# Expert weights in 4 KB runs, hidden sums chunk by chunk, a second tile's work in seven pieces

## The chip, the cores and the metric

One core of a Trainium2 chip runs the whole kernel in one launch. The metric is the time of the program on the device in microseconds, as the median of several runs. TensorE (PE) multiplies, ScalarE (ACT), VectorE (DVE) and GpSimd (POOL) do the rest, SP issues most loads; the five engines run their own queues in order and meet at semaphores.

## The reference

One layer over 1024 latent tokens and 256 context tokens, width 1024. Attention and a gated token mixer come first (they are not touched). Then a mixture of experts (MoE): each token goes to 2 of 16 experts, and

```python
for e in range(N_EXPERTS):                              # 16
    hid = silu(t @ w1[e]) * (t @ w3[e])                 # w1, w3: 1024 x 512
    out = out + gate[:, e:e + 1] * (hid @ w2[e])        # w2: 512 x 1024
```

All inputs are float32. Each expert has 6 MB of weights.

## The kernel before, in words

**Split operands.** A float32 product is made as three matmuls (`mm3`, lines 85 to 88): the operand's part `hi`, rounded by a copy on ACT, and the rest `lo`, which a subtraction gives, combined as hi x hi, hi x lo and lo x hi. So each weight is converted: `e_hi` (line 941, ACT) and `e_lo` (line 946, DVE or POOL).

**Chunks.** An expert's weights come in six chunks of 1 MB, numbered g = 6e + c. Chunks 0 to 3 hold 512 rows of w1 and w3, 256 columns of each, so that (c // 2) is the half `f` of the hidden columns and (c % 2) the half of the rows; a run in memory is 1 KB. Chunks 4 and 5 are w2, in runs of 4 KB. There are seven buffers for raw chunks (`raw`) and six for converted ones (`chi`, `clo`). `e_conv` converts one half of a chunk (1024 columns) at a time; when the second half is done, the next load into that buffer is issued on SP. Some second halves, and both of chunk 7, go to POOL.

**Tiles.** A routing stage writes each expert's list of tokens; `cr[e]` holds their number in registers of all engines (`count`, line 1462). A first tile of up to 128 tokens is always computed. If there are more, a second tile is computed, as a full one (over 192 tokens) or as a half one, whose `hi` and `lo` parts stand side by side in one stationary operand, which makes two matmuls of three (`half_h`, `half_y`). The last expert may have a third tile (`more`).

**One tile.** `gather` (POOL) fetches the tokens' rows; `x_split` transposes them on PE in blocks of 128 consecutive columns (line 1345) and splits them; `h_mm(e, j, f)` adds up one half of the hidden columns over all eight row blocks, 24 matmuls (ACT and DVE then make the hidden part); `h_T` transposes the hidden part; `y_mm` makes 24 matmuls with w2; `y_out` scales and scatters with an add (POOL, line 1388; a half tile at line 1451).

**Order.** The MoE's order is written out by hand for every engine (`manual_schedule`, lines 1534 to 1586). For an expert: the second tile's x (`x_more`, jumped over when there is none; the jump is recorded at line 1564), `h_mm` of half 0, the gather of the next expert's second tile, two conversions, the rest of the second tile as one piece (`more1`, jumped over at line 1528), then half 1 of the first tile, the next expert's x, and the first tile's y. Conversions stand between these. PSUM has four banks for `yb`, two for the hidden sums and two (`pst`) for the transposes. A jump is one compare and branch on every engine; a piece that is jumped over leaves behind it, on each engine that had work in it, an event that adds up the semaphore steps left out.

Of the kernel before, what the change touches and what calls it, by code (L numbers as in the profile page):

```python
# [39 lines left out]
def hybrid_layer_kernel(ctx, tc, a, out):  # L40
# [887 lines left out]
    def e_conv(g, i, eng=None):  # L928
        if g >= CH:
            return  # L930
        e_hi(g, i)
        if eng is None:
            eng = nc.gpsimd if g == 7 or i == 1 and (g == 6 or g >= 2 * 6 and g % 6 in (0, 5)) else nc.vector
        e_lo(g, i, eng)

    def e_hi(g, i):
        sl = slice(i * 1024, (i + 1) * 1024)
        if g == 7:
            nc.vector.tensor_copy(chi[g % NS][:, sl], raw[slot_of(g)][:, sl])
        else:  # L940
            nc.scalar.activation(chi[g % NS][:, sl], raw[slot_of(g)][:, sl], AF.Copy)  # L941

    def e_lo(g, i, eng):
        sl = slice(i * 1024, (i + 1) * 1024)
        r, hi, lo = raw[slot_of(g)], chi[g % NS], clo[g % NS]
        eng.tensor_tensor(lo[:, sl], r[:, sl], hi[:, sl].bitcast(F32), op=ALU.subtract)  # L946
        if i == 1:
            e_load(g + NR if g > 1 else g + 3)
# [215 lines left out]
    for t in range(NT - 1):  # L1164
# [12 lines left out]
        if t >= 5:  # L1177
            e_conv(t - 5, 0)
            e_conv(t - 5, 1)
# [51 lines left out]
    def x_part(src, w, first, last, ks):  # L1231
        for k in ks:
            nc.tensor.matmul(xg[k // 4][:, k % 4, :], src[:, k * P:(k + 1) * P], w, start=first and k % 4 == 0, stop=last and k % 4 == 3)
# [73 lines left out]
    def wk(e, c, k):  # L1307
        g = 6 * e + c
        n = 512 if c < 4 else 1024
        return chi[g % NS][:, k * n:(k + 1) * n], clo[g % NS][:, k * n:(k + 1) * n]  # L1310
# [9 lines left out]
    def bank4(j):  # L1320
        return bank(j, pst).rearrange("p (a n) -> p a n", a=4)
# [5 lines left out]
    hA = ep.tile([P, 256], F32, name="hA")  # L1327
    hB = ep.tile([P, 256], F32, name="hB")
# [9 lines left out]
    def x_split(j):  # L1338
        xg = (sc_f, xgi, xg2)[min(j, 2)]
        hi, lo = (xTi, xT0)[min(j, 1)]  # L1340
        for q in range(2):
            tr = bank4(j)
# [7 lines left out]
    def h_mm(e, j, f, hook=None):  # L1350
        hi, lo = (xTi, xT0)[min(j, 1)]
        po = bank(j, psh)
        for k in range(KD):
            wh, wl = wk(e, 2 * f + k // 4, k % 4)
            mm3(po, hi[:, k, :], lo[:, k, :], wh, wl, k == 0, k == KD - 1)
            if hook is not None and k == hook[0]:
                hook[1]()
        h = (hA, hB)[min(j, 1)]
        nc.scalar.activation(h, po[:, 0:256], AF.Silu)
        nc.vector.tensor_tensor(h, h, po[:, 256:512], op=ALU.mult)  # L1360

    def h_T(j, f):
        hi, lo = hTs[min(j, 1)]
        h = (hA, hB)[min(j, 1)]
        tr = bank4(j)
        for i in range(2):
            nc.tensor.transpose(tr[:, i, :], h[:, i * P:(i + 1) * P], ident)  # L1367
        sl = slice(f * 2, f * 2 + 2)
        nc.scalar.activation(hi[:, sl, :], tr[:, 0:2, :], AF.Copy)
        nc.vector.tensor_tensor(lo[:, sl, :], tr[:, 0:2, :], hi[:, sl, :].bitcast(F32), op=ALU.subtract)  # L1370

    def y_mm(e, j, k0, k1):
        hi, lo = hTs[min(j, 1)]
        if k0 == 0:
            yss[j] = [bank(1, psy) for _ in range(2)]
        for k in range(k0, k1):
            wh, wl = wk(e, 4 + k // 2, k % 2)
            for i in range(2):
                sl = slice(i * 512, (i + 1) * 512)
                mm3(yss[j][i], hi[:, k, :], lo[:, k, :], wh[:, sl], wl[:, sl], k == 0, k == 3)  # L1380

    def y_out(e, j):
# [20 lines left out]
    def half_x(j):  # L1403
        xg = (xgi, xg2)[j - 1]
        for q in range(2):
            tr = bank4(1)
            for i in range(4):
                k = q * 4 + i
                nc.tensor.transpose(tr[:, i, 0:HP], xg[0:HP, k * P:(k + 1) * P], ident[0:HP, 0:HP])
            half_split(xT0[0][:, q * 4:q * 4 + 4, :], tr)  # L1410

    def half_h(e, j, f, hook=None):
        po = bank(1, psy)
        for k in range(KD):
            wh, wl = wk(e, 2 * f + k // 4, k % 4)
            nc.tensor.matmul(po, xT0[0][:, k, :], wh, start=k == 0, stop=False)
            nc.tensor.matmul(po, xT0[0][:, k, :], wl, start=False, stop=k == KD - 1)
            if hook is not None and k == hook[0]:
                hook[1]()
        s = xg2[0:HP, f * 512:(f + 1) * 512]  # L1420
        half_sum(s, po)
        h = hB[0:HP, :]
        nc.scalar.activation(h, s[:, 0:256], AF.Silu)
        nc.vector.tensor_tensor(h, h, s[:, 256:512], op=ALU.mult)

    def half_hT(f):
        tr = bank4(1)
        for i in range(2):
            nc.tensor.transpose(tr[:, i, 0:HP], hB[0:HP, i * P:(i + 1) * P], ident[0:HP, 0:HP])
# [259 lines left out]
```

## Time and profile before

| what | value |
|---|---|
| median of 3 runs (lowest, highest) | 1068.88 us (1066.27, 1072.99) |
| the profiled execution: its time, its span | 1073.15 us, 1071.3 us |
| busy in the span: PE, DVE, ACT, POOL | 1004.6, 735.4, 536.3, 381.6 us |
| mean granted TensorE clock | 0.984 of full speed |
| moved by DMA | 255.26 MB, mean 238 GB/s |
| MoE: first hidden matmul, last matmul | 606.3 us, 1052.8 us |

By the timeline experts 1, 3 to 9 and 14 have one tile; 10, 11, 13 and 15 have a full second one, 0, 2 and 12 a half second one, and 15 a half third one as well. PE's busy time contains the overlap of a matmul's filling with the one before it: a matmul of 512 columns is recorded with 0.39 us, but the next starts 0.23 us later. So gaps are read from the starts. A share of busy time is a mean over stages with different limits; the MoE is read by itself.

### The profile page before, as it was taken

The page shows a single profiled execution, that of the slowest core. Times are in us where ns is not written, and L with a number is a line of the kernel's source. Part 1 is how long each engine was busy: PE and PEld are TensorE (multiplying, and loading weights), DVE is VectorE, ACT ScalarE, POOL GpSimd, SP SyncE. Part 2 cuts the span into 40 slices and gives each one's busy share as a digit, 9 for nine tenths or more (in the row PEclk, how much of TensorE's full clock was granted, in tenths as well). Part 3 has the DMA queues.
Part 4 walks back from the last instruction along what each step waited for, and adds up shares of the span by engine and source line. Part 5 has one row for each costly group of instructions (what it writes and reads, how often), then busy time and mean ns, then how long its engine had stood idle before and what let it go on. Part 6 is the DMA issues. An engine that isn't in the chain of part 4 may idle for free. (4 is left out here: it accounts for less than half of the span.)

```text
span 1071.3 us, 15841 instructions
## 1 busy us (share of the span) xinstructions
PE 1004.6 (94%) x5161; PEld 816.6 (76%) x5161; DVE 735.4 (69%) x1478; ACT 536.3 (50%) x1024; POOL 381.6 (36%) x311
## 2 busy tenths in 40 slices
PE   9999899999999999999999888999998999999992
PEld 4688787876888989988888766777776888787771
DVE  2677658874627989967776858688888654765821
ACT  4643125243527989854322437476676543554611
POOL 1130321232302565641223554435645423243510
PEclk9999999999999999999999999999999999999997
DMA  9793605876757797959342698799999996886431
GB/s 325 271 316 134 200 1 177 287 237 243 252 210 263 253 352 265 322 182 324 122 149 80 202 299 287 247 332 353 346 360 353 343 294 201 292 257 194 131 60 16
DMA packets 138118, 255.26 MB, mean 238 GB/s; under 512 B 10310, under 2 KB 86726, under 8 KB 137994
## 3 DMA queue, kind: packets, MB, share of 16 engines
q1 hardware_dynamic: 122876, 201.57, 55.7%
q0 software_dynamic: 15120, 52.19, 16.1%
q8 instruction: 60, 0.98, 0.4%
q14 instruction: 62, 0.51, 0.2%
HBM read 210.45 MB, written 43.29 MB: 237 GB/s over the span
## 5 line engine op out<-in xcount | busy, mean ns | idle before, releaser
L946 DVE TENSOR_TENSOR clo<-raw,chi 128x1024 fp32r<-128x1024 f32 x140 | 174.2, 1291 | 18.8 <-ACT chi L941 17.7
L941 ACT ACTIVATE chi<-raw 128x1024 fp32r<-128x1024 f32 x166 | 162.6, 1049 | 1.5 <-DMA raw<-in_w 1.3
L86 PE MATMUL po<-whi,hhi 128*128 128x512 f32 x352 | 146.0, 415 | 0.0
L87 PE MATMUL po<-wlo,hhi 128*128 128x512 f32 x352 | 139.6, 397 | 0.0
L88 PE MATMUL po<-whi,hlo 128*128 128x512 f32 x352 | 139.3, 396 | 0.0
L1388 POOL DMA_INDIRECT out<-xb,lt x20 | 58.0, 2899 | 152.0 <-DVE xb L1387 152.0
L86 PE MATMUL b<-chi,yhi 128*128 128x512 f32 x256 | 104.7, 409 | 7.0 <-PEq L1528 4.1
L88 PE MATMUL b<-chi,ylo 128*128 128x512 f32 x256 | 101.7, 397 | 2.0 <-DVE ylo L1348 1.6
L87 PE MATMUL b<-clo,yhi 128*128 128x512 f32 x256 | 101.3, 396 | 0.0
L83 POOL TENSOR_TENSOR ss<-ss,nhalf 128x1 f32<-128x1 f32 (+1 forms) x36 | 46.0, 1276 | 144.2 <-DVE ss L82 144.0
L946 POOL TENSOR_TENSOR clo<-raw,chi 128x1024 fp32r<-128x1024 f32 x26 | 75.2, 2899 | 52.1 <-ACT chi L941 27.8
L86 PEld LDWEIGHTS po<-whi,hhi 128*128 128x128 f32 x352 | 66.7, 189 | 16.6 <-issue 2.6
L87 PEld LDWEIGHTS po<-wlo,hhi 128*128 128x128 f32 x352 | 66.8, 190 | 16.0 <-issue 2.4
L88 PEld LDWEIGHTS po<-whi,hlo 128*128 128x128 f32 x352 | 66.7, 189 | 15.9 <-DVE hlo L218 0.3
L86 PEld LDWEIGHTS b<-chi,yhi 128*128 128x128 f32 x256 | 48.4, 189 | 23.4 <-issue 8.4
L86 PE MATMUL yb<-chi,hhi 128*128 128x512 f32 x160 | 65.7, 411 | 0.0
L88 PE MATMUL yb<-chi,hlo 128*128 128x512 f32 x160 | 62.8, 393 | 0.0
L87 PE MATMUL yb<-clo,hhi 128*128 128x512 f32 x160 | 62.6, 391 | 0.0
L88 PEld LDWEIGHTS b<-chi,ylo 128*128 128x128 f32 x256 | 48.5, 190 | 14.1 <-DVE ylo L1348 2.1
L770 DVE TENSOR_TENSOR PT<-tr,PT 128x384 fp32r<-128x384 f32 (+1 forms) x128 | 56.4, 483 | 3.3 <-ACT PT L764 3.2
L87 PEld LDWEIGHTS b<-clo,yhi 128*128 128x128 f32 x256 | 48.5, 189 | 9.6
L572 DVE CUSTOM_DVE_ANT_0 S<-S,bt 128x640 f32<-128x640 f32 x64 | 52.7, 824 | 4.2 <-DMA bt<-in_btab 3.9
(316 smaller groups left out, 2343.7 us busy)
## 6 DMA issues: line engine op xcount, KB each, us to landing
raw<-in_w SPq DMA_DIRECT2D x104, 512.0 KB, 8.2
raw<-in_w SPq DMA_DIRECT2D x27, 1024.0 KB, 9.4
wraw<-in_w_ada SPq DMA_DIRECT2D x32, 512.0 KB, 5.1
v<-vD SPq DMA_DIRECT2D x16, 768.0 KB, 6.3
bt<-in_btab SPq DMA_DIRECT2D x32, 384.0 KB, 6.8
wraw<-in_w_in SPq DMA_DIRECT2D x20, 512.0 KB, 5.4
acc<-in_w SPq DMA_DIRECT2D x18, 512.0 KB, 7.4
wada<-in_w_ada SPq DMA_DIRECT2D x16, 512.0 KB, 6.6
```

The lines of the kernel that those rows point to most:

```text
L83: nc.gpsimd.tensor_tensor(r, r, nhalf[:, :n], op=ALU.pow)
L86: nc.tensor.matmul(po, xh, wh, start=first, stop=False)
L87: nc.tensor.matmul(po, xh, wl, start=False, stop=False)
L88: nc.tensor.matmul(po, xl, wh, start=False, stop=last)
L572: nc.vector.tensor_tensor_reduce(sv, sv, btl[t, h // 2][:, h % 2 * 384:h % 2 * 384 + LK], op0=ALU.add, op1=ALU.max, scale=1.0, scalar=-3e3 ...
L770: nc.vector.tensor_tensor(lo, tr, hi.bitcast(F32), op=ALU.subtract)
L941: nc.scalar.activation(chi[g % NS][:, sl], raw[slot_of(g)][:, sl], AF.Copy)
L946: eng.tensor_tensor(lo[:, sl], r[:, sl], hi[:, sl].bitcast(F32), op=ALU.subtract)
L1388: nc.gpsimd.indirect_dma_start(out=out[:, :], out_offset=bass.IndirectOffsetOnAxis(ap=lt[:, e, j, 0:1], axis=0), in_=y, in_offset=None, co ...
```

## The change

Weights w1 and w3: partition p takes rows 8p to 8p + 7, and chunk c holds two of them (2c and 2c + 1), with all 512 columns, in runs of 4 KB. The hidden sums of both halves `f` then need all four chunks, and they are taken chunk by chunk, six matmuls for each half. So row block k of x consists of every eighth column, and the transposes read x so (`cols`). A chunk is converted whole (2048 columns) by ACT and DVE, chunk 7 of each six in two halves; POOL converts nothing any more but one half of chunk 3, ahead of the MoE (line 1289, as before). The second tile of an expert is taken in seven pieces, each with its own jump: its x, its hidden sums after each chunk of the first tile (four pieces), its hidden transposes, and its y. For expert 0 its x and hidden sums are one piece. A third tile (`alone`) uses the same parts in an order of its own.

```diff
-                eng.dma_start(r.rearrange("p (k n) -> p k n", k=4)[:, :, i * 256:(i + 1) * 256],
-                                  a[w][e, (c % 2) * 512:(c % 2) * 512 + 512, (c // 2) * 256:(c // 2) * 256 + 256].rearrange("(k p) n -> p k n", p=P))
+                eng.dma_start(r[:, i * 1024:(i + 1) * 1024],
+                              a[w][e].rearrange("(p k) n -> p (k n)", k=KD)[:, c * 1024:(c + 1) * 1024])
...
+    def e_conv(g):
         if g >= CH:
             return
-        e_hi(g, i)
-        if eng is None:
-            eng = nc.gpsimd if g == 7 or i == 1 and (g == 6 or g >= 2 * 6 and g % 6 in (0, 5)) else nc.vector
-        e_lo(g, i, eng)
+        e_hi(g, None)
+        e_lo(g, None, nc.vector)
...
+    def w13(e, f, k):
+        g = 6 * e + k // 2
+        return [w[g % NS].rearrange("p (m k n) -> p m k n", m=2, k=2)[:, :, k % 2, f * 256:(f + 1) * 256] for w in (chi, clo)]
+
+
+    def cols(x, k):
+        return x.rearrange("p (n k) -> p k n", k=KD)[:, k, :]
...
-                nc.tensor.transpose(tr[:, i, :], xg[:, k * P:(k + 1) * P], ident)
+                nc.tensor.transpose(tr[:, i, :], cols(xg, k), ident)
...
+    def h_part(e, j, half, f, chunks):
         hi, lo = (xTi, xT0)[min(j, 1)]
+        for k in range(2 * chunks[0], 2 * chunks[-1] + 2):
+            if k == 0 and j != 1:
+                pos[j, f] = bank(j, psh)
+            po = pos[j, f]
+            wh, wl = w13(e, f, k)
+            if half:
+                nc.tensor.matmul(po, hi[:, k, :], wh, start=k == 0, stop=False)
+                nc.tensor.matmul(po, hi[:, k, :], wl, start=False, stop=k == KD - 1)
+            else:
+                mm3(po, hi[:, k, :], lo[:, k, :], wh, wl, k == 0, k == KD - 1)
+        if chunks[-1] == 3:
...
+            nc.scalar.activation(h, s[:, 0:256], AF.Silu)
+            nc.vector.tensor_tensor(h, h, s[:, 256:512], op=ALU.mult)
...
+    def alone(e, j, half):
+        for c in range(3):
+            for f in range(2):
+                h_part(e, j, half, f, [c])
+        h_part(e, j, half, 0, [3])
+        h_T(e, j, half, 0)
+        h_part(e, j, half, 1, [3])
+        y_mm(e, j, half, 0)
+        h_T(e, j, half, 1)
+        for k in range(1, 4):
+            y_mm(e, j, half, k)
+        y_out(e, j, half)
...
+    def expert(e):
+        g0 = 6 * e
+
+        def second(f, *a):
+            with tc.If(cr[e] > P):
+                with tc.If(cr[e] > P + HP) as c:
+                    f(False, *a)
+                with c.Else():
+                    f(True, *a)
...
+        def second_T(half):
+            for f in range(2):
+                h_T(e, 1, half, f)
+
+        def second_y(half):
+            for k in range(4):
+                y_mm(e, 1, half, k)
+            y_out(e, 1, half)
...
+        if e:
+            second(second_x)
+            gather_more(e + 1)
+        for c in range(3):
+            if e or c:
+                conv(4 + c if e else 3 + c)
+            if e and c == 2:
+                e_hi(g0 + 7, 0)
+            chunk(0, False, c)
+            if e:
+                second(second_h, [c])
+        h_part(e, 0, False, 0, [3])
+        if e:
+            e_lo(g0 + 7, 0, nc.vector)
+        h_part(e, 0, False, 1, [3])
+        if e:
+            second(second_h, [3])
+        else:
+            second(second_xh)
+            gather_more(1)
+            conv(6)
+            e_hi(7, 0)
+            e_lo(7, 0, nc.vector)
+        h_T(e, 0, False, 0, bank(1, psy))
+        if e + 1 < E:
+            x_split(0)
+        if e + 2 < E:
+            gather(e + 2, 0)
+        y_mm(e, 0, False, 0)
+        h_T(e, 0, False, 1)
+        second(second_T)
+        e_hi(g0 + 7, 1)
+        e_lo(g0 + 7, 1, nc.vector)
+        conv(8)
+        for k in range(1, 4):
+            y_mm(e, 0, False, k)
+        y_out(e, 0, False)
+        yss[1] = [bank(1, psy) for _ in range(2)]
+        if e == E - 1:
+            with tc.If(cr[e] > P * 2):
+                gather(e, 2)
+        second(second_y)
+        conv(9)
...
     for e in range(E):
         if e + 1 < E:
-            x_split(0)
...
+            count(e + 1)
+        expert(e)
```

## Rows read from the trace of the kernel before

**Rows 1.** Windows by stage: length, busy time by engine, clock, DMA share, GB/s

```profile
700.00:820.00 120.00, 112.26 (x507) 87.16 (x506) 103.05 (x109) 83.73 (x110) 63.93 (x24) 1.00 1.06 348
820.00:840.00 20.00, 17.53 (x76) 13.90 (x75) 12.88 (x17) 10.97 (x16) 10.74 (x5) 0.91 1.07 352
840.00:983.00 143.00, 141.07 (x658) 113.78 (x656) 86.21 (x111) 70.33 (x104) 48.32 (x23) 1.00 0.82 255
```

**Rows 2.** Waits: ACT conversions for landed weights; TensorE's: total us, times, longest

```profile
  DMA raw<-in_w: 1.3, 1
...
PE b L1367 <- DVE ylo L1348: 5.1, 6, 0.9
PE b L86 <- PEq L1528: 4.1, 2, 2.5
```

**Rows 3.** Timeline of TensorE, one expert with one tile: start, us, instruction

```profile
740.38 0.47 PE L86 MATMUL b<-chi,yhi 128*128 128x512 f32 x1
...
745.58 0.40 PE L87 MATMUL b<-clo,yhi 128*128 128x512 f32 x1
745.82 0.39 PE L88 MATMUL b<-chi,ylo 128*128 128x512 f32 x1
746.36 0.47 PE L86 MATMUL b<-chi,yhi 128*128 128x512 f32 x1
...
752.18 1.03 PE L1345 MATMUL b<-ident,gf 128*128 128x128 f32 x8
...
755.43 0.44 PE L1367 MATMUL b<-ident,hA 128*128 128x128 f32 x2 [0.82 <-DVE ylo L1348]
...
760.17 0.47 PE L86 MATMUL b<-chi,yhi 128*128 128x512 f32 x1
```

**Rows 4.** Lines 1528, 1564, 1462 on TensorE's sequencer: ns min/median/max, first, last start

```profile
L1528 PEldq COMPARE_BRANCH  x15: 65/325/6158, 649.3 to 1004.9; - x15
L1528 PEldq EVENT_SEMAPHORE  x9: 51/51/51, 653.3 to 988.9; - x9
...
L1564 PEldq EVENT_SEMAPHORE  x9: 51/51/51, 645.0 to 982.9; - x9
...
L1462 PEldq TENSOR_LOAD <-cnt x17: 297/304/489, 608.0 to 999.6; - x17
```

**Rows 5.** Scatters: page, part 5, and groups by line

```profile
L1388 POOL DMA_INDIRECT out<-xb,lt x20 | 58.0, 2899 | 152.0 <-DVE xb L1387 152.0
...
L1451 POOL DMA_INDIRECT out<-xb,lt x4 | 5.8, 1447 | 42.0 <-DVE xb L1450 42.0
```

**Rows 6.** VectorE: line 946 by itself; timeline in the expert of rows 3

```profile
L946 DVE TENSOR_TENSOR clo<-raw,chi x140: 1206/1220/3415, 489.3 to 1012.9; 128x1024 fp32r<-128x1024 f32 x140
...
751.96 2.48 DVE L946 TENSOR_TENSOR clo<-raw,chi 128x1024 fp32r<-128x1024 f32 x1 [0.21 <-ACT chi L941]
...
754.69 1.27 DVE L1348 TENSOR_TENSOR ylo<-b,yhi 128x512 fp32r<-128x512 f32 x2
```

**Rows 7.** Timeline of TensorE behind the longest jump

```profile
828.39 0.63 PE L87 MATMUL b<-clo,yhi 128*128 128x512 f32 x1
828.82 0.63 PE L88 MATMUL b<-chi,ylo 128*128 128x512 f32 x1
```

**Rows 8.** Timeline of half tiles: TensorE in expert 12, ACT and TensorE in the third

```profile
928.19 0.31 PE L1429 MATMUL yb<-ident,hB 64*128 64x64 f32 x2 [0.74 <-DVE hB L1424]
...
1047.26 0.59 ACT L1396 ACTIVATE yb<-yb 64x512 f32<-64x512 f32 x1 [0.33 <-PE yb L1417]
...
1049.62 0.30 PE L1429 MATMUL yb<-ident,hB 64*128 64x64 f32 x2 [0.18 <-DVE hB L1424]
1050.67 0.50 PE L1440 MATMUL yb<-chi,hhi 128*128 128x512 f32 x1 [0.75 <-DVE hhi L1401]
```

**Rows 9.** Timeline of VectorE at the end of a half tile's y

```profile
935.00 0.68 DVE L1397 TENSOR_TENSOR yb<-yb 64x512 f32<-64x512 f32 x1 [2.44 <-ACT yb L1396]
...
937.09 0.74 DVE L1450 SCALAR_TENSOR_TENSOR xb<-yb,lt,gf 64x512 f32<-64x512 f32 x1
```

**Rows 10.** Line 1345 on TensorE's weight loads: ns min/median/max

```profile
L1345 PEld LDWEIGHTS b<-ident,gf x120: 138/140/143, 643.7 to 995.5; 128*128 128x128 f32 x120
```

More of the change, by code (lines that the diff above doesn't have):

```diff
@@ L1232, in x_part @@
         for k in ks:
-            nc.tensor.matmul(xg[k // 4][:, k % 4, :], src[:, k * P:(k + 1) * P], w, start=first and k % 4 == 0, stop=last and k % 4 == 3)
+            nc.tensor.matmul(xg[k // 4][:, k % 4, :], src.rearrange("p (n k) -> p k n", k=KD)[:, k, :], w, start=first and k % 4 == 0, stop=last and k % 4 == 3)
     warm = pso.tile([P, 512], F32, tag="po", name="warm")
@@ L1348, in x_split @@
             nc.vector.tensor_tensor(lo[:, sl, :], tr, hi[:, sl, :].bitcast(F32), op=ALU.subtract)
-    def h_mm(e, j, f, hook=None):
+    pos = {}
+    def h_part(e, j, half, f, chunks):
         hi, lo = (xTi, xT0)[min(j, 1)]
[L1352 to L1360, printed above, removed]
@@ new lines, in y_mm @@
+    def y_mm(e, j, half, k):
+        hi, lo = hTs[1 if half else min(j, 1)]
+        if k == 0 and j != 1:
+            yss[j] = [bank(1, psy) for _ in range(2)]
+        wh, wl = wk(e, 4 + k // 2, k % 2)
+        for i in range(2):
+            sl = slice(i * 512, (i + 1) * 512)
+            if half:
+                nc.tensor.matmul(yss[j][i], hi[:, k, :], wh[:, sl], start=k == 0, stop=False)
+                nc.tensor.matmul(yss[j][i], hi[:, k, :], wl[:, sl], start=False, stop=k == 3)
+            else:
@@ L1452, in half_out, with y_out @@
                                      in_=y, in_offset=None, compute_op=ALU.add)
-    def conv2(g):
-        for i in range(2):
-            e_conv(g, i)
+    def y_out(e, j, half):
+        (half_out if half else full_out)(e, j)
     cr = {}
@@ L1498, in one @@
                     gather(e, j + 1)
-            h_mm(e, j, 0)
-            full(e, j)
+            alone(e, j, False)
             if j + 1 < T // P:
@@ L1505, in other @@
             half_x(j)
-            half_h(e, j, 0)
-            half(e, j)
+            alone(e, j, True)
         with tc.If(cr[e] > P * j):
@@ L1515, in more, with second_x, chunk, second_h @@
                 one()
[L1517 to L1529 removed]
+    def expert(e):
[6 more added lines that the diff above has]
+                    f(True, *a)
+        def second_x(half):
+            (half_x if half else x_split)(1)
+        def chunk(j, half, c):
+            for f in range(2):
+                h_part(e, j, half, f, [c])
+        def second_h(half, cs):
+            for c in cs:
+                chunk(1, half, c)
+        def second_xh(half):
+            second_x(half)
+            second_h(half, range(4))
+        def second_T(half):
+            for f in range(2):
+                h_T(e, 1, half, f)
[3 more added lines that the diff above has]
+            y_out(e, 1, half)
+        def conv(*cs):
+            for c in cs:
+                e_conv(g0 + c)
+        for f in range(2):
+            pos[1, f] = bank(1, psy)
+        if e:
[15 more added lines that the diff above has]
+            second(second_h, [3])
+        else:
+            second(second_xh)
[23 more added lines that the diff above has]
+        conv(9)
```

189 lines of the change are left out of this document (48 added, 141 removed).

## The prediction

> **What bounds the kernel now.** I read the busy table by stage first. From 606 us to the last matmul at 1053 us TensorE is nearly always at work, at a granted clock of 1.00 (2.4 GHz), in the stretch of experts with one tile (700 to 820) as in the one with more (840 to 983) [rows 1]. The DMA share is 1.06 in the first, which looks like a limit. It is none: over the whole run ScalarE, which takes each weight chunk first, waited 1.3 us for landed weights [rows 2]. So the MoE is bound by the order of TensorE's own instructions, and the question of each edit is what it does to the gaps there, not to bytes.
>
> Then I followed one expert without a second tile on TensorE, from its first matmul at 740.38 to the next expert's at 760.17: 19.79 us [rows 3]. Seventy-two matmuls about 0.235 us apart are most of it. There are two sorts of gap. One is 0.30 us at each piece that is jumped over: 745.82 to 746.36 is 0.54 us from start to start, where 745.58 to 745.82 is 0.24. The other is 0.82 us before the transposes at 755.43, which wait for VectorE to empty a PSUM bank.
>
> The sequencer's rows explain the first sort [rows 4]. A jumped piece leaves on TensorE's queue an event instruction, nine times at each of lines 1528 and 1564, that adds up the semaphore steps of the matmuls left out. It comes only after TensorE's last matmul is finished, so the array runs empty, however early the branch was decided. The branches at line 1528 take 0.065 to 0.325 us up to the median; the longest took 6.158.
>
> **The change, part by part.** Sixteen first tiles and four full second ones are scattered at line 1388, and four half ones at line 1451 [rows 5]: nine experts (the events' count) have one tile, four a full second tile, three a half one, and the last also a half third one.
>
> *4 KB runs, 2048-wide conversions.* Longer runs shorten transfers that nobody waits for: I take 0, and at most the 1.3 us of rows 2. Two conversions of 1024 columns become one of 2048; what that saves lies beside matmuls.
>
> *No conversion on GpSimd.* Two of an expert's twelve halves go to VectorE, 2 x 1.22 us, and the 1.26 us by which one subtraction overruns (2.48 instead of 1.22) while GpSimd works should go [rows 6]. VectorE is busy 103.05 of 120 us, 17.0 of 19.79, in the stretch with one tile [rows 1], and comes to 18.2. TensorE still covers it, with little to spare: at an expert time under 18.5 us VectorE is next. GpSimd's queue then holds gathers and scatters alone and is never waited for. The overrun delays the eviction that the transposes at 755.43 wait for: six such waits, 5.1 us in all [rows 2], end. **-5.1 us**; 0 if VectorE's added work delays it as much.
>
> *Seven pieces instead of two: the drains.* Before: 18 skips x 0.30 = 5.4 us. After: nine experts x 7 = 63. Where one such expert follows another (six times) the last piece of one and the first of the next share a drain, which leaves 57 x 0.30 = 17.1 us. **+11.7 us.** Between nothing (a short skip lets the array run on) and 0.63 each (a branch of 0.33 behind the drain) I take the measured 0.30, since each new piece holds matmuls too. ScalarE, VectorE, GpSimd and SP pass the same branches; three of the seven pieces hold matmuls alone, the others cost ScalarE and VectorE two more events an expert, under the matmuls.
>
> *What stands behind a drain.* An expert's last piece is now directly ahead of the load of the next count (0.304 us median) and of the branches of the next expert [rows 4]. Today the queue passes them while the array has matmuls in hand. Behind a drain they are exposed: the load and two branches of 0.33, about 1.0 us, nine times less a last expert without a load: **+8.5 us**; 0 if they still pass early, 13 with the pauses between such instructions.
>
> *Long jumps shortened.* Two skips at line 1528 kept TensorE waiting 4.1 us [rows 2], 3.8 above the usual. After the longer the granted clock was 0.91 over 20 us, the array at the 1.2 GHz level for nine matmuls, 0.43 us apart [rows 1, 7]: 9 x 0.19 = 1.7 us. No piece now holds over 24 matmuls and its other branch. **-5.5 us**; 0 if a short piece can meet this too.
>
> *A second tile's tail.* The second tile's last hidden part now ends right before tile zero's transposes. With a full tile, by the order of the two banks that transposes share, those of the second tile wait for the evictions of the next expert's x (two of 0.64 us on VectorE [rows 6], in order behind the activations): about 1.0 us, four times, **+4**. With a half tile both halves of the hidden part end together. The chain that now lies between them, from ScalarE's copy at 1047.26 to the transposes at 1049.62, is 2.4 us [rows 8]. It is passed twice, in order on ScalarE, with tile zero's copies behind it: by the queues' order about 3.25 us idle, where waits of 0.74, 0.18 and some 0.75 stand now: +1.6, twice, **+3.2**. The half third tile, alone, waits for that chain at both halves (2.4, and 2.4 less the 0.9 of four matmuls, instead of 0.9 in all): **+3.0**. At an expert's start 12 matmuls (2.8 us) instead of 24 cover the second x's splits, which stand behind a subtraction of 2.3 us and, after a half tile, behind sums and scalings that run from 935.00 to 937.83 [rows 9]: 1.9 us once, 0.5 twice, **+3**. For these four together the bounds are 0, if all is covered, and 20, if one of these idles also costs clock as in rows 7.
>
> *Expert 0.* It had a half tile's waits and has them again, with two conversions more ahead of tile zero's copies, and expert 1's x comes earlier: 0, from -6 to +6 (a wait of 3.25 us and a clock loss of 1.7 either way, rounded up).
>
> *Transposes of strided columns.* x is now read at every eighth column. Eight transposes take 1.03 us [rows 3], and their weight loads of 0.14 us each run beside them [rows 10]. No row shows a strided read by TensorE. From nothing to a load twice as long that sets the pitch, 8 x (0.28 - 0.10) = 1.4 us for each of 20 tiles, 29 us; I take 0, as the nearest rows hide the load.
>
> Sum: -5.1 + 11.7 + 8.5 - 5.5 + 4 + 3.2 + 3 + 3 = +22.8. The profiled execution took 1073.15 us, 4.3 above the median of the runs; so 1096.0 against its own time is **1092 us** against the median of 1068.88.
>
> On the skips the Trainium skill, "Advanced Engine Details and Errata", section Control Flow Timing, gives about 108 ns for a compare-and-branch; if that were a skip's price, 63 would make an estimated 6.8 us instead of 17.1, and the sum some 10 us less. The rows differ: 0.30 us a skip.
>
> **The rivals.** *Skips covered (faster).* The array runs on through short pieces because the queue is far ahead, and the tails are covered. Then the old 5.4, the 5.1 and the 5.5 us fall away: 1053 us. For it: branches are taken early. Against it: all 18 skips posted the event that waits [rows 4]. With tails and loads covered it decides below 0.27 us a skip (39 more skips at that make up the 10.6 gained). The Trainium skill's figure above would lead here.
>
> *Gains and drains cancel (same).* Drains cost 0.30, but the loads behind them and the tails are hidden: 11.7 - 5.1 - 5.5 = +1.1, 1070 us. Here too belongs that the 4 KB runs do all they say and nobody waits for them.
>
> *Strided reads (slower still).* A weight load that takes longer doubles the pitch of the transposes, 0.10 to 0.20: 8 x 0.10 x 20 = 16 us on the forecast, 1108; 1121 at most. For it: eight stand in a row, with no long matmul to hide a load. Against it: no row shows such a price. The Trainium skill, "Advanced Engine Details and Errata", section SBUF Cachelines, says that accesses which each fall in another 16-byte line pay a penalty, as words eight apart do; no run so far shows it.
>
> **The numbers.** Forecast 0.47 and strided reads 0.15 make slower 0.62; cancel 0.21; covered 0.17. Within 1% means 1058 to 1080, about what a measurement of this kernel tells from no change. The range 1060 to 1112 leaves out most of the covered case and the upper part of the strided one; the forecast alone is 1080 to 1104.
>
> **What would show it.** An expert without a second tile should take about 21 us (19.8 - 0.8 + 4 x 0.30 + 1.0), with five steps of 0.5 us from start to start inside and one of over 1 us at its end; 63 events on TensorE's queue at the jumping line; no wait of TensorE for VectorE's split of the next x; no fall of the clock past expert 0. The forecast is wrong if those experts take under 19.8 us, if steps at skips are under 0.4 us, or if eight transposes of x take over 1.3 us.

## The result: 5% slower, and where the 50 us lie

The changed kernel takes 1121.93 us (median of 4 runs, 1118.36 to 1123.87) against 1070.1 for the kernel before: a ratio of 1.0483, interval 1.0438 to 1.0528. Measured again later, beside other runs, it is 1.0478 (1.0427 to 1.0530). The forecast was 1092 with a range up to 1112: the direction was right, the size was not, and the time lies outside the range. Where 23 us more were forecast, 52 came by the medians.

The profiled executions have spans of 1121.2 and 1071.3 us, 50 apart. Laid side by side by TensorE's timeline, from the first H matmul of one expert to that of the next, the difference splits so:

| Stretch | before | after | difference | forecast |
|---|---|---|---|---|
| to the last routing matmul of token tile 6 | 590.0 | 587.2 | -2.8 | 0 |
| from there to expert 0's first H matmul | 16.28 | 22.84 | +6.6 | 0 |
| expert 0 | 39.2 | 49.8 | +10.6 | 0 |
| nine experts with one tile | 185.2 | 195.4 | +10.2 | +9.6 |
| six later experts with a second tile | 206.9 | 227.7 | +20.8 | +10.2 |
| the half third tile | 15.2 | 21.1 | +5.9 | +3.0 |
| behind the last matmul | 18.5 | 17.2 | -1.3 | 0 |

(+9.6 is 11.7 + 8.5 - 5.5 - 5.1, and +10.2 is 4 + 3.2 + 3.) The part on which the prediction spent most words came out within 0.6 us. The parts that it put at zero, and what it left out at the second and third tiles, make the error. Expert 0 does not repeat: in a second profile of the changed kernel it takes 45.9 us, which makes +6.7 of the +10.6.

The windows of the changed kernel, answering to [rows 1] (length, busy time by engine, clock, DMA share, GB/s):

```profile
700.00:820.00 120.00, 107.55 (x474) 80.33 (x473) 98.72 (x92) 75.68 (x79) 15.33 (x12) 1.00 0.90 305
840.00:1042.00 202.00, 189.02 (x849) 149.12 (x848) 131.34 (x132) 101.64 (x112) 35.28 (x21) 0.98 0.75 240
```

TensorE is busy 107.55 of 120 us where it was 112.26. GpSimd is nearly free of work, as the change says, and the DMA share has fallen from 1.06 to 0.90. The loads wait for the experts: in the whole run ScalarE waited 0.6 us for landed weights.

One expert with one tile, the answer to [rows 3] (start, us, instruction, idle time before and its releaser):

```profile
782.25 0.50 PE L86 MATMUL b<-chi,yhi 128*128 128x512 f32 x1 [1.28 <-PEq L1518]
...
784.92 0.39 PE L88 MATMUL b<-chi,ylo 128*128 128x512 f32 x1
785.46 0.47 PE L86 MATMUL b<-chi,yhi 128*128 128x512 f32 x1
...
795.12 1.06 PE L1355 MATMUL b<-ident,gf 128*128 128x128 f32 x8
...
801.92 0.39 PE L88 MATMUL yb<-chi,hlo 128*128 128x512 f32 x1
803.61 0.50 PE L86 MATMUL b<-chi,yhi 128*128 128x512 f32 x1 [1.30 <-PEq L1518]
```

782.25 to 803.61 is 21.36 us. 784.92 to 785.46 is 0.54 from start to start: a gap of 0.30, the drain at a skipped piece, five times in the expert. At its end two skipped pieces and the load of a count stand together, and 801.92 to 803.61 is 1.69 us. The wait for the subtraction of the next x [rows 2] is gone. The sequencer at the jumping line, the answer to [rows 4], has the 63 events that were counted out, and no branch over 0.42 us:

```profile
L1518 PEldq COMPARE_BRANCH  x108: 65/208/419, 617.1 to 1069.4; - x108
L1518 PEldq EVENT_SEMAPHORE  x63: 51/51/51, 659.3 to 1039.6; - x63
```

The subtractions, now all of an expert's on VectorE, are 2048 wide but for the halves named in the change. They overrun less than in [rows 6]: the longest takes 2.82 us where the median is 2.28. The line by itself (ns min/median/max):

```profile
L951 DVE TENSOR_TENSOR clo<-raw,chi x96: 1210/2284/2824, 487.7 to 1048.0; 128x2048 fp32r<-128x2048 f32 x69, 128x1024 fp32r<-128x1024 f32 x27
```

### The profile page after: what moved, and what is told of

It is laid out like the page before. It is cut to its first block, busy times and chain, and to the rows that moved or that the text cites. A ratio compares the mean times of both kernels' runs of the same rounds, so it can differ in the third digit from the quotient of the medians.

```text
span 1121.2 us, 16267 instructions
## 1 busy us (share of the span) xinstructions
PE 1030.0 (92%) x5161; PEld 829.6 (74%) x5161; DVE 751.0 (67%) x1428; ACT 538.9 (48%) x947; POOL 277.2 (25%) x280
## 5 line engine op out<-in xcount | busy, mean ns | idle before, releaser
L951 DVE TENSOR_TENSOR clo<-raw,chi 128x2048 fp32r<-128x2048 f32 (+1 forms) x96 | 191.0, 2008 | 24.0 <-ACT chi L945 12.0
L945 ACT ACTIVATE chi<-raw 128x2048 fp32r<-128x2048 f32 (+1 forms) x97 | 158.3, 1664 | 36.6 <-PE yb L88 15.2
L1426 POOL DMA_INDIRECT out<-xb,lt x20 | 35.8, 1788 | 198.0 <-DVE xb L1425 95.8
L83 POOL TENSOR_TENSOR ss<-ss,nhalf 128x1 f32<-128x1 f32 (+1 forms) x36 | 45.9, 1275 | 144.2 <-DVE ss L82 144.1
L88 PE MATMUL yb<-chi,hlo 128*128 128x512 f32 x160 | 65.1, 407 | 1.2 <-DVE hlo L1405 1.2
L1383 ACT ACTIVATE h<-b 128x256 f32<-128x256 f32 x32 | 12.3, 385 | 96.8 <-PE b L88 96.8
L1344 POOL DMA_INDIRECT gf<-hfD,lt x15 | 14.7, 982 | 165.5 <-PE b L1355 159.8
```

The costliest lines, as they stand in the source:

```text
L83: nc.gpsimd.tensor_tensor(r, r, nhalf[:, :n], op=ALU.pow)
L88: nc.tensor.matmul(po, xl, wh, start=False, stop=last)
L945: nc.scalar.activation(part(chi[g % NS], g, i), part(raw[slot_of(g)], g, i), AF.Copy)
L951: eng.tensor_tensor(lo, r, hi.bitcast(F32), op=ALU.subtract)
L1344: nc.gpsimd.indirect_dma_start(out=xg[0:n, :], out_offset=None, in_=hfD[:, :], in_offset=bass.IndirectOffsetOnAxis(ap=lt[0:n, e, j, 0:1], ...
L1426: nc.gpsimd.indirect_dma_start(out=out[:, :], out_offset=bass.IndirectOffsetOnAxis(ap=lt[:, e, j, 0:1], axis=0), in_=y, in_offset=None, co ...
```

## The experiments

The theory after the result: (a) the skipped pieces cost what was forecast; (b) before expert 0, the one-hot matmuls that gather its first tile read every eighth column, and the load of expert 1's count now stands ahead of H; (c) expert 0 loses by a late gather and by conversions put ahead of copies; (d) the third tile's gather is issued too late. Rivals: VectorE alone is too slow for the conversions; strided transposes cost in every expert; 4 KB runs matter. Of the versions of the changed kernel that undo one thing, only the one with five pieces has an interval clear of the changed kernel's first one, and that barely. For the others the traces have to decide: experts 4 to 8 repeat to about 0.1 us from profile to profile where an edit leaves them alone, but expert 0 takes 45.7 to 52.0 us in seven profiles in which its conversions are as in the changed kernel.

### Strided one-hot matmuls

```diff
+  if e == 0:
+      eng.dma_start(r[:, i * 1024:(i + 1) * 1024].rearrange("p (k n) -> p k n", k=2),
+                    a[w][e, c * 256:c * 256 + 256, :].rearrange("(k p) n -> p k n", p=P))
-  matmul(xg.., src.rearrange("p (n k) -> p k n", k=KD)[:, k, :], w, ..)
+  matmul(xg.., src[:, k * P:(k + 1) * P], w, ..)
```

> Changed kernel, but expert 0 keeps the order of rows of before: its w1/w3 come in 2 KB runs, and the 48 one-hot matmuls that gather its first tile (and its second tile's transposes) read x in contiguous columns. Theory 'strided one-hot matmuls': 16 of them take 4.0 us in the changed kernel against 1.95 in the kernel before, so with contiguous columns the load of a weight is 192 ns again instead of 335 and the start of expert 0's H matmuls comes 3.5 to 5 us earlier; the whole about 4 us less than the changed kernel, 1118 us (ratio 1.045). Rival 'the wait for the count before expert 0 is what delayed its start': the matmuls get shorter, the start of H does not move, 1122 us (1.048).

Measured: ratio 1.0459 (1.0406 to 1.0512). (The transposes of expert 0's second tile read contiguous columns too; that part of the edit is not shown.) The same for every expert, so that no x is read with a stride and all w1/w3 come in 2 KB runs:

> Changed kernel with the old order of rows in every expert: w1/w3 in 2 KB runs (the kernel before had 1 KB, the changed one 4 KB) and every x read in contiguous columns, in the one-hot matmuls and in the transposes. Theory 'only the one-hot matmuls pay for the stride': the same time as the run with expert 0 alone in the old order, within 2 us (1118 us, ratio 1.045), although the weight load of a transpose falls from 193 to about 140 ns. Rival 'the strided transposes slow every expert': another 0.2 us an expert and more, 1115 us or less. Rival 'the 4 KB runs are worth something': slower than that run by more than 3 us, with waits of TensorE for chunks that have not landed.

Measured: 1.0405 (1.0360 to 1.0451). The intervals overlap with each other and with the changed kernel's; the traces decide. First the changed kernel, then the version with contiguous columns everywhere: weight loads by line (ns min/median/max), then the timeline.

```profile
L1237 PEld LDWEIGHTS xg<-sel,hf x16: 334/336/337, 597.2 to 600.7; 128*128 128x128 f32 x16
L1355 PEld LDWEIGHTS b<-ident,gf x120: 186/193/207, 638.2 to 1033.1; 128*128 128x128 f32 x120
```

```profile
597.28 3.98 PE L1237 MATMUL xg<-sel,hf 128*128 128x128 f32 x16
...
610.04 0.47 PE L86 MATMUL b<-chi,yhi 128*128 128x512 f32 x1 [2.16 <-DVE cnt L1284]
```

```profile
L1237 PEld LDWEIGHTS xg<-sel,hf x16: 192/192/193, 595.9 to 597.6; 128*128 128x128 f32 x16
L1355 PEld LDWEIGHTS b<-ident,gf x120: 138/141/143, 634.0 to 1028.5; 128*128 128x128 f32 x120
```

```profile
595.99 1.95 PE L1237 MATMUL xg<-sel,hf 128*128 128x128 f32 x16
...
606.53 0.47 PE L86 MATMUL b<-chi,yhi 128*128 128x512 f32 x1 [2.19 <-DVE cnt L1284]
```

With a stride of eight words a weight load takes 336 instead of 192 ns and 16 matmuls 3.98 instead of 1.95 us. From the routing matmul of tile 6 to H it is 22.8 us with the stride, 18.8 and 18.6 without, 16.3 before: about 4.1 us are the stride, and most of the other 2.4 is the wait of 2.2 for the count, which both versions keep. The transposes' loads also lengthen (193 for 141 ns), but eight still take 1.06 us against 1.03, and one-tile experts take 21.4 to 21.6 us with and without the stride. So the strided transposes cost nothing that the experts' lengths show, and 2 KB runs lose nothing against 4 KB.

### The load of the count

```diff
   for k in range(1, 4): y_mm(e, 0, False, k)
+  if e + 2 < E: count(e + 2)
   y_out(e, 0, False)
...
   count(0)                 # ahead of the experts
+  count(1)
...
-  if e + 1 < E: count(e + 1)   # head of each expert
```

> Changed kernel with the register load of the count of expert e+2 put between the last y matmuls of expert e's first tile and the output, where matmuls are queued, instead of the head of the next expert, where the engine has just drained behind a piece that was jumped over. Theory 'the boundary load is exposed': each of 15 boundaries shrinks from 1.4 us to about 0.3, up to -16 us, and 8 or more of it stays in the whole: 1106 to 1114 us (ratio 1.033 to 1.041). Rival 'the load blocks wherever it stands, since the sequencer does not run far enough ahead': the 1.1 us appear at the new place, no change, 1122 us.

Measured: 1.0435 (1.0392 to 1.0479). The boundary between one-tile experts in this version's timeline:

```profile
796.04 0.39 PE L88 MATMUL yb<-chi,hlo 128*128 128x512 f32 x1
797.30 0.50 PE L86 MATMUL b<-chi,yhi 128*128 128x512 f32 x1 [0.88 <-PEq L1518]
```

1.26 us from start to start instead of 1.69. The load was 0.42 us of the boundary (idle time 0.88 instead of 1.30), not 1.1: the rest stays without it. What stands there is the two skipped pieces and the branch around the gather for the next expert's second tile. The wait of 2.2 us before expert 0 went as well, since this version loads expert 1's count earlier. The expected 8 us and more did not come: the nine one-tile experts lose 3.4 us together, which with the 2.2 makes 5.6, and the ratio moved by about 5 us, with intervals that overlap.

### Five pieces instead of seven

```diff
-  if e: second(second_h, [c])
+  if e and c == 1: second(second_h, [0, 1])
...
-  second(second_h, [3])
+  second(second_h, [2, 3])
```

> Changed kernel with five pieces of the second tile instead of seven: its H matmuls of chunks 0 and 1 in one piece behind chunk 1, those of chunks 2 and 3 in one behind chunk 3. Theory 'a skipped piece costs its drain of 0.30 us, whatever is in it': two pieces less in each of 9 one-tile experts with pieces are 9 x 2 x 0.30 = 5.4 us, an expert falls from 21.4 to 20.8 us, and experts with a second tile lose as many drains: 1114 to 1117 us (ratio 1.041 to 1.044). Rival 'the drains are covered elsewhere, the extra time of a one-tile expert lies in the conversions': an expert stays at 21.4 us, 1122 us.

Measured: 1.0381 (1.0331 to 1.0432), about 10 us less. First H matmuls of two one-tile experts that follow each other:

```profile
802.41 0.50 PE L86 MATMUL b<-chi,yhi 128*128 128x512 f32 x1 [1.29 <-PEq L1518]
...
822.99 0.50 PE L86 MATMUL b<-chi,yhi 128*128 128x512 f32 x1 [1.28 <-PEq L1518]
```

20.58 us instead of 21.36: two pieces less give 0.78, not 0.60. Beyond the one-tile experts, expert 10 gave 1.0, expert 13 2.6 and expert 15 with its third tile 3.6. What goes there is a wait for the split of the second tile's x, which in the changed kernel stands after the first 12 matmuls of the experts 10, 13 and 15 (the last 1.21 us) and not in this version; 10 and 13 in the changed kernel:

```profile
872.41 0.47 PE L86 MATMUL yb<-chi,xhi 128*128 128x512 f32 x1 [0.88 <-DVE xlo L1358]
...
985.50 0.47 PE L86 MATMUL yb<-chi,xhi 128*128 128x512 f32 x1 [2.29 <-DVE xlo L1358]
```

### No pieces at all

```diff
   def second(f, *a):
+      return
```

> Changed kernel without the pieces of the second tile (the tokens of the second tiles are left out of the sum; the gathers of their x stay), so that nothing is jumped over within an expert. Theory 'the pieces are what a one-tile expert pays for': without them it takes 18.3 to 19.0 us instead of 21.4 (six gaps of 0.30 and most of the 1.3 at the boundary go), with no idle time of TensorE above 0.4 us in it. Rival 'part of the 21.4 us lies in the new order of the work itself, in conversions on VectorE and strided reads': 19.8 us or more, with waits for VectorE.

Measured: 961.94 us in a single run, and the lengths of its experts 1 to 14 are what counts: 19.15 to 19.24. The wait that is left in each, by its timeline:

```profile
758.42 0.44 PE L1399 MATMUL yb<-ident,h 128*128 128x128 f32 x2 [0.81 <-DVE h L1384]
...
777.65 0.44 PE L1399 MATMUL yb<-ident,h 128*128 128x128 f32 x2 [0.80 <-DVE h L1384]
```

So the pieces cost a one-tile expert 21.4 - 19.2 = 2.2 us: five drains of 0.30 and 1.46 at the boundary, less this 0.80, which the drains hide. The expert of before, less its two drains, is 19.79 - 0.60 = 19.19: the new order of the work by itself gains nothing and loses nothing. The length lies between the two theories' numbers, nearer to the first, but the wait of 0.80 is above the 0.4 that the first allowed.

### Expert 0

```diff
   for c in cs:
-      e_conv(g0 + c)
+      for i in (0, 1) if g0 + c in (3, 4, 5) else (None,):
+          e_hi(g0 + c, i); e_lo(g0 + c, i, nc.vector)
```

> Changed kernel with the subtractions of expert 0's own chunks 4 and 5 on VectorE in halves of 1024 columns again, nothing else. In the changed kernel GpSimd's addition of the slot lists took 2.54 us (0.74 in the kernel before) and its issue of the second tile's gather 2.73 us (0.98), both while VectorE ran 2048-wide subtractions, and TensorE then waited 5.3 us for that gather. Theory 'GpSimd stands still for the length of a VectorE instruction beside it': with halves both come down by 0.8 us or more each, the gather lands 1.5 to 3.5 us earlier and expert 0 shrinks from 49.8 us to 46 to 48.5. Rival 'GpSimd shares with VectorE in proportion, however long one instruction is': addition and issue stay at 2.5 to 2.7 us, the wait at 5.3, the time at 1122 us (ratio 1.048).

Measured: 1.0430 (1.0394 to 1.0465). GpSimd's addition took 1.23 us, its issue of the gather 1.64, TensorE's wait was 1.71. Expert 0 took 47.9 us, inside the spread of the changed kernel, so that its length decides nothing here. Moving the conversions:

```diff
   second(second_xh); gather_more(1)
-  conv(6); e_hi(7, 0); e_lo(7, 0, nc.vector)
...
   second(second_T)
+  if e == 0: conv(6); e_hi(7, 0); e_lo(7, 0, nc.vector)
```

> Changed kernel with expert 0's conversion of expert 1's chunks 0 and half of 1 moved from ahead of its first tile's copies of h transposed to behind the second tile's. Theory 'the first tile's copies stand behind two conversions on ScalarE and VectorE': the waits of 3.7 and 1.2 us for the copies of h transposed in expert 0 go, with the slow stretch of TensorE behind them, and expert 0 shrinks from 49.8 to 43 to 46 us; the whole 4 to 6 us less (ratio 1.043). Rival 'the conversions are only moved, and expert 1's first chunk is late instead': expert 0 shrinks and expert 1 grows by the same, or the transposes of the next x wait, 1122 us (1.048).

Measured: 1.0430 (1.0385 to 1.0474). And the changed kernel once more, as a base:

> The changed kernel once more, beside the other runs of this call, as the base for the versions of it: 1118 to 1124 us (ratio 1.044 to 1.050).

Measured: 1.0478 (1.0427 to 1.0530). GpSimd and TensorE in expert 0 of the changed kernel, first profile:

```profile
614.18 2.54 POOL L1294 TENSOR_TENSOR lt<-lt,lt 128x256 int32<-128x256 int32 x1 [3.62 <-DMA lt<-lD]
617.00 2.73 POOL L1344 DMA_INDIRECT y<-hfD,lt  x1 [0.27 <-POOL lt L1294]
```

```profile
626.63 1.12 PE L1447 MATMUL b<-ident,y 64*128 64x64 f32 x8 [5.30 <-DMA y<-hfD,lt]
...
643.59 0.79 PE L86 MATMUL yb<-chi,hhi 128*128 128x512 f32 x1 [3.69 <-ACT hhi L1404]
...
646.03 0.80 PE L88 MATMUL yb<-chi,hlo 128*128 128x512 f32 x1 [1.22 <-DVE hlo L1405]
```

The second profile of the same kernel, where the addition met VectorE at another moment:

```profile
610.53 0.86 POOL L1294 TENSOR_TENSOR lt<-lt,lt 128x256 int32<-128x256 int32 x1 [3.10 <-DMA lt<-lD]
612.06 2.33 POOL L1344 DMA_INDIRECT y<-hfD,lt  x1 [0.67 <-POOL lt L1294]
```

There TensorE did not wait for the gather at all and expert 0 took 45.9 us instead of 49.8. With 2048-wide subtractions the addition took 0.79 to 2.89 us over ten profiles and the issue always 2.27 to 2.75; in the two versions of the changed kernel with halves 0.74 to 1.23 and 1.18 to 1.64. The Trainium skill, "SBUF — State Buffer", section Who interferes with whom, says that a VectorE instruction with two inputs in SBUF contends with a GpSimd instruction that reads SBUF, and that the pair of ports they share is an exclusive lock. For the addition the trace agrees: what GpSimd loses follows the length of VectorE's instruction and the moment. The issue of the gather stretches with the width in the same way. The moment differs from run to run, which goes with the wide spread of the changed kernel (1112 to 1126 us).

The issue is not all that makes this gather late. From its start to the landing of its data it took, in the kernel before, the changed kernel, the version with halves, and the version with halves and the undoings at the end of this section (us at the end of each line):

```profile
y<-hfD,lt POOLq DMA_INDIRECT x1, 4.3
y<-hfD,lt POOLq DMA_INDIRECT x1, 9.5
y<-hfD,lt POOLq DMA_INDIRECT x1, 8.5
y<-hfD,lt POOLq DMA_INDIRECT x1, 4.5
```

Without the issue itself these are 3.3, 6.8, 6.9 and 3.3 us. So the halves by themselves shortened the issue and left the transfer as long as it was. It took 4.1 to 4.5 us to land in all five profiles of the kernel before and its versions, and 7.6 us or more in all the others but the last. Why the transfer takes longer there, beside other loads or for another reason, was not tried.

Expert 0 of the kernel before has such a wait too, in its second tile's y, ahead of matmuls at the lower clock:

```profile
637.59 0.79 PE L1440 MATMUL yb<-chi,hhi 128*128 128x512 f32 x1 [3.50 <-DVE hhi L1401]
```

In the version with moved conversions the waits of 3.69 and 1.22 us shrink to one of 0.82, with no transposes at the lower clock behind it. Expert 0 takes 37.2 us, against 45.9 in the profile of the changed kernel that did not wait for the gather either. But part returns:

```profile
634.63 0.51 PE L86 MATMUL yb<-chi,hhi 128*128 128x512 f32 x1 [0.82 <-ACT hhi L1404]
...
660.78 0.44 PE L1399 MATMUL yb<-ident,h 128*128 128x128 f32 x2 [1.75 <-DVE h L1384]
```

Expert 1 grows by 2.0 us, as VectorE reaches its work later. Expert 2 grows by 2.5 us; it has the same waits as in the changed kernel but ran at a granted clock of 0.86 instead of 0.95.

### The third tile's gather

```diff
   if e:
       second(second_x)
       gather_more(e + 1)
+  if e == E - 1:
+      with tc.If(cr[e] > P * 2): gather(e, 2)
...
-  if e == E - 1:
-      with tc.If(cr[e] > P * 2): gather(e, 2)
   second(second_y)
```

> Changed kernel with the gather of the last expert's third tile issued at the head of the last expert, behind its second tile's split, instead of just ahead of its last piece. Theory 'the gather comes too late': the wait of 4.0 us for it goes, and the stretch of lower clock behind it (0.50 granted): the last expert with its third tile shrinks from 62.7 us to 56 to 59 (ratio 1.043 to 1.045). Rival 'the third tile is bound by its own chain of transposes and copies': the 4.0 us appear as other waits of that tile, 1122 us (1.048).

Measured: 1.0415 (1.0358 to 1.0471). The third tile in the changed kernel, then in this version:

```profile
1082.89 1.11 PE L1447 MATMUL b<-ident,yb 64*128 64x64 f32 x8 [3.97 <-DMA yb<-hfD,lt]
1084.70 0.80 PE L1372 MATMUL yb<-chi,xhi 128*128 128x512 f32 x1 [0.70 <-DVE xhi L1439]
...
1096.05 0.31 PE L1399 MATMUL b<-ident,yb 64*128 64x64 f32 x2 [2.39 <-DVE yb L1384]
```

```profile
1077.19 1.07 PE L1447 MATMUL b<-ident,yb 64*128 64x64 f32 x8 [0.41 <-DVE xb L1425]
1078.95 0.50 PE L1372 MATMUL yb<-chi,xhi 128*128 128x512 f32 x1 [0.70 <-DVE xhi L1439]
```

The wait goes, and the H matmuls behind it no longer start at the lower level: 0.50 us for the first instead of 0.80. Expert 15 with its third tile takes 57.0 us instead of 62.7. The third tile alone, from its transposes on, takes 18.9 us, 3.7 more than before: the forecast for its chain was 3.0.

### No conversion on GpSimd, alone

```diff
-  eng = nc.gpsimd if g == 7 or i == 1 and (..) else nc.vector
+  eng = nc.vector
...
-  if g == 7: nc.vector.tensor_copy(chi ..)
-  else: nc.scalar.activation(chi ..)
+  nc.scalar.activation(chi ..)
```

> Kernel before, with the one part of the change that moves all conversions from GpSimd to VectorE (their second half on VectorE too, chunk 7's first half on ScalarE), its order and its pieces of work as they were. Theory as in the prediction: 5.1 us less than the kernel before (ratio 0.995), no expert waits for a conversion on VectorE. Rival 'VectorE alone is too slow for the conversions, and this is what the changed kernel pays in its one-tile experts': ratio 1.01 or more, with waits of TensorE for VectorE's subtractions.

Measured: 1.0048 (1.0023 to 1.0073), 5 us slower instead of 5 faster. Experts 4 to 8 take 20.5 to 20.7 us instead of 19.8, experts 1 and 3 grow by 1.7 and 3.0:

```profile
782.19 0.44 PE L1364 MATMUL b<-ident,hA 128*128 128x128 f32 x2 [1.15 <-DVE ylo L1345]
...
799.50 0.66 PE L1342 MATMUL b<-ident,gf 128*128 128x128 f32 x4 [0.16 <-DVE hlo L1367]
```

The wait for the x subtraction that should have ended [rows 2, 3] grew from 0.82 to 1.15. To see whether it is the bank or VectorE's queue, the second half of h was given a bank of y, first in all experts, then from expert 1 on, then with all conversions on VectorE:

```diff
-  tr = bank4(j)
+  tr = bank4(j or own)     # own: second half of h (in the first version in all experts)
```

> Kernel before with one thing of the changed kernel's order: the transposes of h do not wait for a bank that the split of the next x holds (the second half of h goes to one of the four banks of y). In the kernel before a one-tile expert waits 0.86 us there for VectorE. Theory 'this wait is on the path': 0.5 to 0.86 us in each of 10 or more experts, 5 to 10 us less than before (ratio 0.991 to 0.995). Rival 'the wait moves to the copy of h behind the same subtraction on VectorE': the same time (0.998 to 1.002).

Measured: 1.0012 (0.9983 to 1.0041). Experts 3 to 8 take 19.2 to 19.4 us instead of 19.8 to 20.2, but expert 0 took 44.8: its y waited 2.35 us for a bank held by the second tile's split, and ran at the lower clock after it. Experts 1 and 9 grew by 2.1 and 1.4.

> Kernel before with the second half of h transposed into a bank of y, from expert 1 on only (in the version for all experts, expert 0's first y matmuls waited 2.4 us for a bank that the second tile's split held, and lost what nine one-tile experts gained, 0.6 us each). Theory 'the bank wait is on the path': one-tile experts at 19.2 us instead of 19.8, expert 0 as before, 4 to 6 us less than before (ratio 0.994 to 0.997). Rival 'what the experts gain is given back in experts 1 and 10, where the wait for the bank covered another': 0.998 to 1.002.

Measured: 0.9977 (0.9960 to 0.9993). This is the version that beats both kernels, the one before by 2 us. Experts 4 to 8 gain 0.6 us each and expert 9 gains 3.4, but expert 3 gives back 1.7 and expert 10 gives back 5.2, with one wait of 3.7 us for a conversion on ScalarE. Not all of this is the bank: the longer jump of [rows 2], 2.5 us in expert 9 of the kernel before, did not come in this profile.

> The same, and no conversion on GpSimd. By itself this part of the change made the kernel before 5 us slower, with 1.15 us of wait for the subtraction of the next x where there were 0.86, and a new wait of 0.16 to 0.39 us for the copy of h. Theory 'the conversions on VectorE cost only through that bank': with the bank free, this run equals the run without the GpSimd part or is up to 5 us faster (ratio 0.990 to 0.997). Rival 'VectorE's queue itself is what TensorE waits for': one-tile experts stay at 20 us or more, ratio 1.002 to 1.008.

Measured: 0.9989 (0.9971 to 1.0008). Neither theory holds whole. One-tile experts take 19.9 us, so VectorE's longer queue does cost, 0.7 us each, without the bank: over 40 us of this version the waits of TensorE for VectorE are (us in total, times, longest)

```profile
PE yb L1364 <- DVE hA L1357: 1.1, 2, 0.5
...
PE b L1342 <- DVE hlo L1367: 0.2, 1, 0.2
```

But the whole is no slower than before by its interval: experts 3 and 10, where the version with GpSimd lost (21.9 us, and 28.2 to the second tile's part), take 19.9 and 23.4 here. Why the stalls there come in one version and not in the other was not tried.

### All undoings together

> Changed kernel with five undoings together: w1/w3 in 2 KB runs and x in contiguous columns, the count loaded among queued matmuls, five pieces instead of seven, expert 0's early conversions behind its second tile, the third tile's gather early. If each lies on the path by itself: 4 (one-hot matmuls) + 2 (count before expert 0) + 4 (boundaries) + 9 (pieces) + 8 (expert 0, less what experts 1 and 2 give back) + 6 (third tile) = 33 us, 1089 us (ratio 1.018). Rival 'they hide one another': 1100 us or more (1.03). Below 1070 it should not come, since five skipped pieces in nine experts and the longer tails of second tiles stay.

Measured: 1.0209 (1.0155 to 1.0262).

> The changed kernel with the five undoings, and expert 0's conversions in halves as well. In the run with five, TensorE still waited 3.5 us for the second tile's gather in expert 0 and ran at a lower clock behind it. Theory 'the late gather is GpSimd's standing still beside VectorE': the wait falls below 2 us and expert 0 from 42.6 to 37 to 40 us; the whole 1089 to 1093 us (ratio 1.016 to 1.020). Rival 'its flight is bound by the weight loads beside it': the wait stays at 3 us or more, 1095 us (1.021).

Measured: 1.0138 (1.0116 to 1.0160): 36 of the 52 us are gone. Its interval and that of the version without the halves just touch. GpSimd and TensorE in its expert 0:

```profile
612.20 0.74 POOL L1294 TENSOR_TENSOR lt<-lt,lt 128x256 int32<-128x256 int32 x1 [2.10 <-DMA lt<-lD]
613.71 1.18 POOL L1344 DMA_INDIRECT y<-hfD,lt  x1 [0.78 <-POOL lt L1294]
```

```profile
618.33 0.68 PE L1447 MATMUL b<-ident,y 64*128 64x64 f32 x8 [0.52 <-DMA y<-hfD,lt]
```

The gather's wait is 0.5 us and expert 0 takes 37.9 us, less than before's 39.2. What remains by the lengths of the experts is 0.8 us in each of the experts 4 to 8 (6.0 in all nine with one tile), 5.0 us in the experts 2 and 10 to 13, and 6.9 in expert 15 with its third tile.

## Why the prediction was wrong

The sum failed at what it put at zero or left out: expert 0 (+10.6), the stretch ahead of it (+6.6) and the late gather of the third tile (5.7). The terms that it did work out came near, one of them for the wrong reason.

**Drains, exposed load, long jumps: right.** 0.30 us a skip, 63 events, experts of "about 21 us", a boundary "of over 1 us": all as forecast, and the nine experts' sum is +10.2 where +9.6 was said. At a boundary 1.46 us were lost where a drain of 0.30 and about 1.0 were said; of the parts, the load cost 0.42 us by the run that moves it, where 0.30 was priced, and a second event and the branch around the next gather were left out.

**No conversion on GpSimd: wrong in sign.** "TensorE still covers it, with little to spare" failed: in the order of before it costs 5 us. In the changed order the x wait does end, for another reason (h has a bank of its own, and x's split stands behind it); without pieces a wait of 0.80 us for VectorE takes its place, and the drains hide that. The near agreement of the nine experts' sum is therefore partly luck: a gain for the wrong reason, -0.8 us an expert, stood in for the term.

**Strided columns: right for the transposes, and the wrong place.** "No row shows a strided read by TensorE" led me to cost the 20 tiles' transposes only. The 48 one-hot matmuls in the diff read x with the same stride, have no spare time beside their weight loads, and cost 4.1 us. The penalty that the Trainium skill, "Advanced Engine Details and Errata", section SBUF Cachelines, names was the warning. In these runs both loads are longer with the stride (336 for 192 ns, 193 for 141), and time is lost only at the one-hot matmuls, whose pitch doubled.

**Expert 0: the step that failed most.** It was put at 0, with -6 to +6, and made +10.6 (+6.7 in the second profile). The prediction named the "two conversions more ahead of tile zero's copies", which are 3.7 and 1.2 us of wait with transposes and y matmuls at the lower clock behind them, but set a gain beside them that did not come: with these conversions moved the expert takes 37.2 us. It missed that the gather could come late. 2048-wide subtractions, costed at nothing as they lie "beside matmuls", hold up GpSimd's addition and issue, and the transfer behind them takes longer as well, which stays unexplained; the wait for the gather is up to 5.3 us and differs from run to run. The count ahead of H (2.2 us) was seen at later boundaries and forgotten at this one.

**A second tile's tails: the four terms about right, other costs left out.** The four terms were +13.2 with a bound of 20, and the two rows of the table hold +26.7. TensorE's idle times in the changed kernel, less those of the kernel before, and the length of the third tile when its gather is early, put the four at about 13: the split of the second x 4.4 (forecast 3), the tails of full tiles 3.1 (4), of half tiles 1.7 (3.2), and the third tile 3.7 (3). Tails of a full tile (expert 10) and of a half one (expert 2):

```profile
895.67 0.41 PE L1399 MATMUL b<-ident,yb 128*128 128x128 f32 x2 [0.57 <-DVE hlo L1405]
```

```profile
705.73 0.51 PE L86 MATMUL yb<-chi,hhi 128*128 128x512 f32 x1 [1.88 <-ACT hhi L1404]
...
708.62 0.31 PE L1399 MATMUL b<-ident,yb 64*128 64x64 f32 x2 [0.69 <-DVE hlo L1405]
```

What the sum lacked is the third tile's late gather, 5.7 by the run that moves it, a DMA of a moved step that was not followed past the queue; about 2.6 from a fall of the clock in expert 12 (36.2 us at 0.91 granted; 33.5 at 1.00 in the second profile); and some 5 us that no wait named here explains and that were not tried singly. "No fall of the clock past expert 0" was wrong too: 0.98 granted over 840 to 1042.

**The rivals.** Skips were not covered; nothing cancelled; strided reads decided nothing at the 20 tiles. That the measured 1122 us is the upper end of the strided rival, 1121, is chance: eight transposes take 1.06 us, under the 1.3 that was its sign. The time came out beyond the range since each term of zero was taken as a zero of the sum and not as a bound.

## What to carry to other kernels

A piece that is jumped over costs a drain each time (TensorE runs empty), 0.3 to 0.4 us here, so merge pieces before shortening them, and let no register load stand behind one. When a layout changes, list every reader of the tensor, those before the loop too; when a step moves, list its DMAs. Widening an instruction on VectorE lengthens what GpSimd must wait for beside it, so look who else is on the path at that moment, in the first iteration above all.

## What the hardware showed

A weight load of 128 columns eight words apart took 336 ns for one-hot matmuls (192 contiguous) and 193 ns for transposes (141). Eight transposes took 1.06 us with the longer load and 1.03 without, so it was hidden there; the pitch of the one-hot matmuls went from 0.12 to 0.25 us with it. GpSimd's issue of a gather, not only its arithmetic, stretches beside long VectorE subtractions: 2.3 to 2.75 us beside 2048 columns, 1.2 to 1.6 beside 1024 in the versions of the changed kernel, 0.98 in the kernel before. The event left by a skipped piece makes TensorE run empty: the next matmul starts 0.54 us after the last one instead of 0.24.
